# ReGLU MLP on one core: the first two chunks' first matmuls interleaved, and the second matmuls two chunks behind

## The chip, the cores and the metric

The kernel runs on one core of a Trainium2 chip. The metric is the device time of one execution in microseconds (us). The time before is the median of 6 runs, 356.47 us (355.37 to 356.92).

## What is computed

The input x has 16 x 256 = 4096 rows of 512 numbers. All inputs and the output are float32.

```python
h = x @ w1                              # w1: 512 x 4096
gate, value = np.split(h, 2, axis=-1)   # 2048 columns each
h = np.maximum(gate, 0) * value
return (h @ w2).astype(np.float32)      # w2: 2048 x 512
```

## The kernel before, in words

The 4096 rows are cut into 8 chunks of 512 rows (`T_CHUNK`, `NC`), each chunk into 4 blocks of 128 rows (`NB`). All matmuls are in bf16. The work of a chunk has two parts.

- MM1 (`mm1_pair`, L120 to L148) makes the hidden layer transposed, 128 hidden columns at a time. A pair is 4 matmuls of 128x512 into `val_ps` (L124) and 4 into `gate_ps` (L132); ScalarE copies `val_ps` to SBUF (L140), and VectorE makes max(gate, 0) * value and writes it as bf16 into `g_sb` (L141). A chunk has 16 pairs, 128 matmuls.
- MM2 (`mm2_block`, L150) makes one block of 128 output rows: 16 matmuls of 128x512 into `out_ps` (L154), a copy by ScalarE (L162), a store issued by SP (L163). A chunk has 4 blocks, 64 matmuls. The very last block is split into two halves of 256 columns (L166 to L180).

MM1 needs x transposed (`xt_sb`). It comes in two ways. For the first three chunks (`N_PE`), SP loads float32 blocks (`xf_sb`, L74), TensorE transposes each block in 4 pieces against a float32 identity (L102), and VectorE copies the result to `xt_sb` as bf16 (L105); this is `pe_transpose_block`. The four blocks of chunk 0 stand ahead of all MM1; the eight of chunks 1 and 2 are placed one behind each of the pairs 1 to 8 of chunk 0 (`pe_xpose_after_pair`, L192). For the chunks 3 to 7, POOL issues a DMA that casts the chunk to bf16 in DRAM (L109), and SP issues 4 transposing DMAs (L114). The cast is traced two chunks ahead of its use, the transposes one chunk ahead.

The weights are loaded and cast to bf16 by DMAs that POOL issues: w1 in ten pieces (L81; four of 256 columns, gate and value in turn, then six of 512), then w2 in four (L95). The w1 piece that holds the value columns of pairs 0 and 1 is the second. POOL makes the two identities (L53 to L56) ahead of these DMAs. Twelve small transposes of the bf16 identity (L68) go to TensorE at the very start.

The order of work: within a chunk all 16 pairs, then MM2 of the chunk before (L214). So MM2 of the last chunk comes at the end. The code is traced in this order, and a planner (the tile framework) puts each engine's instructions into the order in which they are issued: program order is the priority, but an instruction whose inputs are there earlier, by the planner's own reckoning, may be put ahead. It also places all semaphores. Each engine then works in its order; a wait holds everything behind it on that engine. A tile pool with n buffers makes the tile n later wait until the earlier one is read: `xtpool` and `gpool` have 3 buffers, the PSUM pools 2 per tile.

```python
for c in range(NC):
    ...
    for pr in range(NH):
        mm1_pair(xt_tiles[c], g_tiles[c], pr)
        if c == 0 and pr in pe_xpose_after_pair:
            k, b = pe_xpose_after_pair[pr]
            pe_transpose_block(xt_tiles[k], xf_tiles[k], b)
    if c >= 1:
        for b in range(NB):
            mm2_block(g_tiles[c - 1], c - 1, b)
```

Of the kernel before, what the change touches and what calls it, by code (L numbers as in the profile page):

```python
# [11 lines left out]
def kernel(  # L12
# [7 lines left out]
    nc = tc.nc  # L20
    P = 128
    dt = mybir.dt
    fp32 = dt.float32
    bf16 = dt.bfloat16

    x2 = x.flatten_outer_dims()
    out2 = out.flatten_outer_dims()
    T, D = x2.shape
    D2, J = w1.shape
    H, DO = w2.shape  # L30
    assert D2 == D and J == 2 * H and DO == D

    ND = D // P
    NH = H // P
    T_CHUNK = 512
    NC = T // T_CHUNK
    NB = T_CHUNK // P
    N_PE = 3
    N_WARMUP = 12

    const = ctx.enter_context(tc.tile_pool(name="const", bufs=1))
    wpool = ctx.enter_context(tc.tile_pool(name="wpool", bufs=1))
    xfpool = ctx.enter_context(tc.tile_pool(name="xfpool", bufs=N_PE))
    xtpool = ctx.enter_context(tc.tile_pool(name="xtpool", bufs=3))
    gpool = ctx.enter_context(tc.tile_pool(name="gpool", bufs=3))
    vpool = ctx.enter_context(tc.tile_pool(name="vpool", bufs=3))
    opool = ctx.enter_context(tc.tile_pool(name="opool", bufs=4))
    dram = ctx.enter_context(tc.tile_pool(name="dram", bufs=NC, space=bass.MemoryType.DRAM))
    ps_mm1 = ctx.enter_context(tc.tile_pool(name="ps_mm1", bufs=2, space=bass.MemoryType.PSUM))
    ps_mm2 = ctx.enter_context(tc.tile_pool(name="ps_mm2", bufs=2, space=bass.MemoryType.PSUM))  # L50
    ps_xt = ctx.enter_context(tc.tile_pool(name="ps_xt", bufs=2, space=bass.MemoryType.PSUM))

    ident_bf = const.tile([P, P], bf16)  # L53
    make_identity(nc, ident_bf)
    ident_f32 = const.tile([P, P], fp32)
    make_identity(nc, ident_f32)  # L56

    w1_sb = wpool.tile([P, ND, J], bf16)
    w2_sb = wpool.tile([P, NH, DO], bf16)

    w1_v = w1.rearrange("(dc p) j -> p dc j", p=P)
    w2_v = w2.rearrange("(hc p) n -> p hc n", p=P)
    x_v = x2.rearrange("(c b p) d -> c p b d", p=P, b=NB)
    out_v = out2.rearrange("(c b p) d -> c p b d", p=P, b=NB)

    warm = ps_xt.tile([P, ND, P], bf16, name="ps_xt")
    for i in range(N_WARMUP):
        nc.tensor.transpose(warm[:, i % ND, :], ident_bf, ident_bf)  # L68

    xf_tiles = {}  # L70
    for c in range(N_PE):
        xf = xfpool.tile([P, NB, D], fp32, name="xf_sb")
        for b in range(NB):
            nc.sync.dma_start(out=xf[:, b, :], in_=x_v[c, :, b, :])  # L74
        xf_tiles[c] = xf

    JQ = J // 8
    HQ = JQ // 2

    def load_w1_cols(j0, width):  # L80
        nc.gpsimd.dma_start(  # L81
            out=w1_sb[:, :, j0:j0 + width],
            in_=w1_v[:, :, j0:j0 + width],
        )
# [2 lines left out]
    load_w1_cols(4 * JQ, HQ)  # L87
    load_w1_cols(0 * JQ + HQ, HQ)
    load_w1_cols(4 * JQ + HQ, HQ)
    for q in (1, 2, 3):  # L90
        load_w1_cols(q * JQ, JQ)
        load_w1_cols((4 + q) * JQ, JQ)

    for h0 in range(0, NH, 4):
        nc.gpsimd.dma_start(  # L95
            out=w2_sb[:, h0:h0 + 4, :], in_=w2_v[:, h0:h0 + 4, :]
        )

    def pe_transpose_block(xt_tile, xf_tile, b):
        ps = ps_xt.tile([P, ND, P], fp32, name="ps_xt")  # L100
        for dc in range(ND):
            nc.tensor.transpose(  # L102
                ps[:, dc, :], xf_tile[:, b, dc * P:(dc + 1) * P], ident_f32
            )
        nc.vector.tensor_copy(out=xt_tile[:, :, b * P:(b + 1) * P], in_=ps)  # L105

    def emit_cast_chunk(c):
        xbf = dram.tile([T_CHUNK, D], bf16, name="x_bf16")
        nc.gpsimd.dma_start(out=xbf, in_=x2[c * T_CHUNK:(c + 1) * T_CHUNK, :])  # L109
        return xbf  # L110

    def emit_transpose_chunk(xbf, xt_tile):
        for dc in range(ND):
            nc.sync.dma_start(  # L114
                out=xt_tile[:, dc, :],
                in_=xbf[:, dc * P:(dc + 1) * P],
                transpose=True,
            )

    def mm1_pair(xt_tile, g_tile, pr):  # L120
        gate_ps = ps_mm1.tile([P, T_CHUNK], fp32, name="gate_ps")
        val_ps = ps_mm1.tile([P, T_CHUNK], fp32, name="val_ps")
        for dc in range(ND):
            nc.tensor.matmul(  # L124
                val_ps,
                w1_sb[:, dc, H + pr * P:H + (pr + 1) * P],
                xt_tile[:, dc, :],
                start=(dc == 0),
                stop=(dc == ND - 1),
            )  # L130
        for dc in range(ND):
            nc.tensor.matmul(  # L132
                gate_ps,
                w1_sb[:, dc, pr * P:(pr + 1) * P],
                xt_tile[:, dc, :],
                start=(dc == 0),
                stop=(dc == ND - 1),
            )
        val_sb = vpool.tile([P, T_CHUNK], fp32, name="val_sb")
        nc.scalar.copy(out=val_sb, in_=val_ps)  # L140
        nc.vector.scalar_tensor_tensor(  # L141
            out=g_tile[:, pr, :],
            in0=gate_ps,
            scalar=0.0,
            in1=val_sb,
            op0=mybir.AluOpType.max,
            op1=mybir.AluOpType.mult,
        )  # L148

    def mm2_block(g_tile, c, b, split_tail=False):  # L150
        if not split_tail:
            out_ps = ps_mm2.tile([P, DO], fp32, name="out_ps")
            for hc in range(NH):
                nc.tensor.matmul(  # L154
                    out_ps,
                    g_tile[:, hc, b * P:(b + 1) * P],
                    w2_sb[:, hc, :],
                    start=(hc == 0),
                    stop=(hc == NH - 1),
                )  # L160
            o_sb = opool.tile([P, DO], fp32, name="o_sb")
            nc.scalar.copy(out=o_sb, in_=out_ps)  # L162
            nc.sync.dma_start(out=out_v[c, :, b, :], in_=o_sb)  # L163
        else:
            DH = DO // 2
            for h in range(2):  # L166
                out_ps = ps_mm2.tile([P, DO], fp32, name="out_ps")
                for hc in range(NH):
                    nc.tensor.matmul(  # L169
                        out_ps[:, h * DH:(h + 1) * DH],  # L170
                        g_tile[:, hc, b * P:(b + 1) * P],
                        w2_sb[:, hc, h * DH:(h + 1) * DH],
                        start=(hc == 0),
                        stop=(hc == NH - 1),
                    )
                o_sb = opool.tile([P, DH], fp32, name="o_sb_half")
                nc.scalar.copy(out=o_sb, in_=out_ps[:, h * DH:(h + 1) * DH])  # L177
                nc.sync.dma_start(
                    out=out_v[c, :, b, h * DH:(h + 1) * DH], in_=o_sb
                )  # L180

    xt_tiles = {}
    g_tiles = {}
    xbf_tiles = {}

    xt_tiles[0] = xtpool.tile([P, ND, T_CHUNK], bf16, name="xt_sb")
    for b in range(NB):
        pe_transpose_block(xt_tiles[0], xf_tiles[0], b)
    for k in range(1, N_PE):
        xt_tiles[k] = xtpool.tile([P, ND, T_CHUNK], bf16, name="xt_sb")  # L190

    pe_xpose_after_pair = {}  # L192
    for k in range(1, N_PE):
        for b in range(NB):
            pe_xpose_after_pair[(k - 1) * NB + b + 1] = (k, b)

    for c in range(NC):
        k = c + 2
        if N_PE <= k < NC:
            xbf_tiles[k] = emit_cast_chunk(k)  # L200
        nxt = c + 1
        if N_PE <= nxt < NC:
            xt_tiles[nxt] = xtpool.tile([P, ND, T_CHUNK], bf16, name="xt_sb")
            emit_transpose_chunk(xbf_tiles[nxt], xt_tiles[nxt])

        g_tiles[c] = gpool.tile([P, NH, T_CHUNK], bf16, name="g_sb")

        for pr in range(NH):
            mm1_pair(xt_tiles[c], g_tiles[c], pr)
            if c == 0 and pr in pe_xpose_after_pair:  # L210
                k, b = pe_xpose_after_pair[pr]
                pe_transpose_block(xt_tiles[k], xf_tiles[k], b)

        if c >= 1:  # L214
            for b in range(NB):
                mm2_block(g_tiles[c - 1], c - 1, b)
            del g_tiles[c - 1]

    for b in range(NB):
        mm2_block(g_tiles[NC - 1], NC - 1, b, split_tail=(b == NB - 1))  # L220


# [28 lines left out]
```

## Time and profile before

| What | Value |
|---|---|
| median of 6 runs | 356.47 us (355.37 to 356.92) |
| the profiled execution | 357.17 us |
| its span, first to last instruction | 355.4 us |
| mean granted TensorE clock | 0.999 |
| MM1 and MM2 matmuls in the kernel | 1536 |
| one MM1 copy on ScalarE (L140) | 586 ns, 128 times |
| one MM1 product on VectorE (L141) | 691 ns, 128 times |
| x blocks loaded by SP | 12, of 256 KB |
| stores of 256 KB by SP, issue to landing | 31, median 2.0 us |
| w1 pieces, issue to landing | 10, median 20.1 us |
| x casts by DMA (L109), issue to landing | 5, 19.6 to 20.0 us |

How to read it: the span is shorter than the execution's own time, which also holds what lies before the first and behind the last instruction. PE is TensorE, PEld its weight loads (beside the matmuls), DVE VectorE, ACT ScalarE, POOL GpSimd, and SP the engine that only issues DMAs. "x12" after a row is the number of instructions. The times of a chain or timeline row are its start and its length in us from the start of the span. A matmul's own duration in the profile (about 380 ns) is longer than the step from one matmul to the next, because matmuls overlap in the array; the steps are what counts. q1 is the queue of the DMAs that SP issues, q0 that of POOL's.

### The profile page before, as it was taken

To read this page: it belongs to the slowest core of one execution; us is meant where nothing else is said; L and a number is where in the kernel's file an instruction comes from. 1 tells how busy PE (TensorE), PEld (TensorE's weight loads), DVE (VectorE), ACT (ScalarE), POOL (GpSimd) and SP (SyncE) were. 2 spreads that over 40 slices of the span, in tenths; PEclk is the share of its full clock that TensorE was granted. 3 is DMA by queue.
4 is the path that set the end of the run, shared out by engine and by line. 5 is a ranking of instruction groups with operands and counts; after the bars stand their busy time and mean duration, and the time that the engine had idled before them with its cause. 6 is when DMAs were issued, how large, how long until landed. Compare 5 with 4: busy or idle time off the path is not lost.

```text
span 355.4 us, 3970 instructions
## 1 busy us (share of the span) xinstructions
PE 342.6 (96%) x1581; PEld 160.7 (45%) x1612; DVE 96.1 (27%) x140; ACT 95.2 (27%) x162; POOL 14.1 (4%) x27
## 2 busy tenths in 40 slices
PE   5599999999999999999999999999999999999996
PEld 4245444444444444444444444444444444444444
DVE  2145434420333104330144203341033301442000
ACT  1022333321333123321333213331233213332111
POOL 8132000000000000000000000000000000000000
PEclk9999999999999999999999999999999999999999
DMA  8999994023000320004100130000200011000212
GB/s 201 280 206 207 229 226 71 1 34 116 30 0 2 89 89 2 0 3 117 59 0 2 39 108 32 1 0 31 89 0 2 0 59 61 0 0 2 89 60 87
DMA packets 24929, 23.31 MB, mean 66 GB/s; under 512 B 11904, under 2 KB 19328, under 8 KB 24832
## 3 DMA queue, kind: packets, MB, share of 16 engines
q0 software_dynamic: 7552, 8.91, 14.5%
q1 hardware_dynamic: 17360, 14.16, 13.2%
q8 instruction: 12, 0.20, 0.2%
q14 instruction: 5, 0.04, 0.0%
HBM read 20.97 MB, written 11.01 MB: 90 GB/s over the span
## 4 chain that ended last, share of the span: by engine, by line
PE 95%; DMA 3%; issue 1%; POOL 0%; ACT 0%; POOLq 0%
PE val_ps L124 31%; PE gate_ps L132 31%; PE out_ps L154 30%; DMA w_sb<-in_w_dram 3%; PE out_ps L169 1%; PE ps_xt L102 1%; POOL w_sb L81 0%; ACT o_sb_half L177 0%; POOL ident_bf masks.py:199 0%; POOL ident_f_92 masks.py:199 0%; POOL ident_f_92 masks.py:197 0%; POOL ident_bf masks.py:197 0%; POOLq L235 0%
## 5 line engine op out<-in xcount | busy, mean ns | idle before, releaser
L141 DVE SCALAR_TENSOR_TENSOR g_sb<-gate_ps,val_sb 128x512 bf16<-128x512 f32 x128 | 88.5, 691 | 221.0 <-PE gate_ps L132 215.8
L124 PE MATMUL val_ps<-xt_sb,w_sb 128*128 128x512 bf16 x502 | 131.6, 383 | 4.1 <-DMA w_sb<-in_w_dram 3.7
L132 PE MATMUL gate_ps<-xt_sb,w_sb 128*128 128x512 bf16 x500 | 131.1, 382 | 0.7
L140 ACT COPY val_sb<-val_ps 128x512 f32<-128x512 f32 x128 | 75.0, 586 | 158.9 <-PE val_ps L124 151.7
L154 PE MATMUL out_ps<-w_sb,g_sb 128*128 128x512 bf16 x487 | 107.7, 379 | 0.5
L124 PEld LDWEIGHTS <-w_sb 128*128 128x128 bf16 x512 | 50.4, 99 | 63.7 <-DMA w_sb<-in_w_dram 4.1
L132 PEld LDWEIGHTS <-w_sb 128*128 128x128 bf16 x512 | 50.5, 99 | 61.5 <-issue 1.9
L154 PEld LDWEIGHTS <-g_sb 128*128 128x128 bf16 x496 | 48.5, 98 | 58.5
L162 ACT COPY o_sb<-out_ps 128x512 f32<-128x512 f32 x31 | 18.2, 586 | 95.0 <-PE out_ps L154 91.2
L102 PE MATMUL ps_xt<-ident_f_92,xf_sb 128*128 128x128 f32 x48 | 9.4, 336 | 2.5 <-DMA xf_sb<-in_x_dram 2.5
L105 DVE CAST xt_sb<-ps_xt 128x512 bf16<-128x512 f32 x12 | 8.2, 685 | 7.9 <-PE ps_xt L102 7.9
L102 PEld LDWEIGHTS ps_xt<-ident_f_92,xf_sb 128*128 128x128 f32 x48 | 7.2, 173 | 5.2 <-DVE xt_sb L105 2.5
L81 POOL DMA_DIRECT2D w_sb<-in_w_dram x10 | 7.6, 785 | 6.1 <-DMA w_sb<-in_w_dram 6.1
L169 PE MATMUL out_ps<-w_sb,g_sb 128*128 128x256 bf16 x32 | 3.7, 273 | 0.0
L169 PEld LDWEIGHTS <-g_sb 128*128 128x128 bf16 x32 | 3.1, 98 | 0.6
L95 POOL DMA_DIRECT2D w_sb<-in_w_dram x4 | 3.0, 740 | 6.6 <-DMA w_sb<-in_w_dram 6.6
L68 PE MATMUL ps_xt<-ident_bf 128*128 128x128 bf16 x12 | 1.5, 312 | 1.5 <-POOL ident_bf masks.py:199 1.5
L68 PEld LDWEIGHTS <-ident_bf 128*128 128x128 bf16 x12 | 1.2, 144 | 1.5 <-POOL ident_bf masks.py:199 1.5
L140 ACT ACT_TABLE_LOAD x1 | 1.3, 1283 | 0.7 <-PEq L235 0.7
L177 ACT COPY o_sb_half<-out_ps 128x256 f32<-128x256 f32 x2 | 0.7, 372 | 2.5 <-PE out_ps L169 2.5
L109 POOL DMA_DIRECT2D x_bf_425<-in_x_dram x1 | 0.5, 532 | 1.8 <-DMA w_sb<-in_w_dram 1.8
L109 POOL DMA_DIRECT2D x_bf_716<-in_x_dram x1 | 0.5, 502 | 2.0 <-DMA w_sb<-in_w_dram 2.0
(11 smaller groups left out, 2.8 us busy)
## 6 DMA issues: line engine op xcount, KB each, us to landing
out_dram<-o_sb SPq DMA_DIRECT2D x31, 256.0 KB, 2.0
w_sb<-in_w_dram POOLq DMA_DIRECT2D x10, 512.0 KB, 20.1
xf_sb<-in_x_dram SPq DMA_DIRECT2D x12, 256.0 KB, 7.8
w_sb<-in_w_dram POOLq DMA_DIRECT2D x4, 256.0 KB, 13.0
x_bf_425<-in_x_dram POOLq DMA_DIRECT2D x1, 512.0 KB, 20.0
x_bf_716<-in_x_dram POOLq DMA_DIRECT2D x1, 512.0 KB, 19.9
x_bf_1012<-in_x_dram POOLq DMA_DIRECT2D x1, 512.0 KB, 19.8
x_bf_1308<-in_x_dram POOLq DMA_DIRECT2D x1, 512.0 KB, 19.6
```

The lines of the kernel that those rows point to most:

```text
L68: nc.tensor.transpose(warm[:, i % ND, :], ident_bf, ident_bf)
L81: nc.gpsimd.dma_start(out=w1_sb[:, :, j0:j0 + width], in_=w1_v[:, :, j0:j0 + width],)
L95: nc.gpsimd.dma_start(out=w2_sb[:, h0:h0 + 4, :], in_=w2_v[:, h0:h0 + 4, :])
L102: nc.tensor.transpose(ps[:, dc, :], xf_tile[:, b, dc * P:(dc + 1) * P], ident_f32)
L105: nc.vector.tensor_copy(out=xt_tile[:, :, b * P:(b + 1) * P], in_=ps)
L124: nc.tensor.matmul(val_ps, w1_sb[:, dc, H + pr * P:H + (pr + 1) * P], xt_tile[:, dc, :], start=(dc == 0), stop=(dc == ND - 1),)
L132: nc.tensor.matmul(gate_ps, w1_sb[:, dc, pr * P:(pr + 1) * P], xt_tile[:, dc, :], start=(dc == 0), stop=(dc == ND - 1),)
L140: nc.scalar.copy(out=val_sb, in_=val_ps)
L141: nc.vector.scalar_tensor_tensor(out=g_tile[:, pr, :], in0=gate_ps, scalar=0.0, in1=val_sb, op0=mybir.AluOpType.max, op1=mybir.AluOpType.mult,
L154: nc.tensor.matmul(out_ps, g_tile[:, hc, b * P:(b + 1) * P], w2_sb[:, hc, :], start=(hc == 0), stop=(hc == NH - 1),)
L162: nc.scalar.copy(out=o_sb, in_=out_ps)
L169: nc.tensor.matmul(out_ps[:, h * DH:(h + 1) * DH], g_tile[:, hc, b * P:(b + 1) * P], w2_sb[:, hc, h * DH:(h + 1) * DH], start=(hc == 0), s ...
```

## The change

- MM1 of the chunks 0 and 1 is traced pair by pair in turn: pair 0 of chunk 0, pair 0 of chunk 1, pair 1 of chunk 0, and so on. All eight blocks of both chunks are transposed by TensorE ahead of it in the program. Chunks 2 to 7 get x by cast and transposing DMAs; the six casts are all traced at the start, behind w1 and ahead of w2, on POOL's queue.
- MM2 follows two chunks behind: chunk c's MM1, then MM2 of chunk c - 2. At the end stand MM2 of chunks 6 and 7.
- The bf16 identity and the twelve small transposes go. Eight matmuls of 128x512 on a zeroed tile take their place; VectorE zeroes it. The float32 identity is made on POOL behind the first four w1 DMAs.
- `mm2_block` is written without the two branches; its matmuls, copies and stores are the same.

The diff, cut to its core:

```diff
-    N_PE = 3
-    N_WARMUP = 12
+    N_JOINT = 2
+    N_WARMUP = 8
...
-    ident_bf = const.tile([P, P], bf16)
-    make_identity(nc, ident_bf)
-    ident_f32 = const.tile([P, P], fp32)
-    make_identity(nc, ident_f32)
...
+    dummy = const.tile([P, DO], bf16)
+    nc.vector.memset(dummy, 0.0)
+    warm_ps = ps_mm2.tile([P, DO], fp32, name="out_ps")
+    for i in range(N_WARMUP):
+        nc.tensor.matmul(warm_ps, dummy[:, :P], dummy, start=True, stop=True)
...
-    warm = ps_xt.tile([P, ND, P], bf16, name="ps_xt")
-    for i in range(N_WARMUP):
-        nc.tensor.transpose(warm[:, i % ND, :], ident_bf, ident_bf)
...
-    for c in range(N_PE):
+    for c in range(N_JOINT):
...
     load_w1_cols(4 * JQ + HQ, HQ)
+
+    ident_f32 = const.tile([P, P], fp32)
+    make_identity(nc, ident_f32)
+
     for q in (1, 2, 3):
         load_w1_cols(q * JQ, JQ)
         load_w1_cols((4 + q) * JQ, JQ)
+
+    xbf_tiles = {}
+    for c in range(N_JOINT, NC):
+        xbf = dram.tile([T_CHUNK, D], bf16, name="x_bf16")
+        nc.gpsimd.dma_start(out=xbf, in_=x2[c * T_CHUNK:(c + 1) * T_CHUNK, :])
+        xbf_tiles[c] = xbf
...
+    for c in range(N_JOINT):
         for b in range(NB):
-            pe_xpose_after_pair[(k - 1) * NB + b + 1] = (k, b)
...
+            pe_transpose_block(xt_tiles[c], xf_tiles[c], b)
+
+    if N_JOINT < NC:
+        xt_tiles[N_JOINT] = xtpool.tile([P, ND, T_CHUNK], bf16, name="xt_sb")
+        emit_transpose_chunk(xbf_tiles[N_JOINT], xt_tiles[N_JOINT])
+
+    for c in range(N_JOINT):
+        g_tiles[c] = gpool.tile([P, NH, T_CHUNK], bf16, name="g_sb")
+    for pr in range(NH):
+        for c in range(N_JOINT):
+            mm1_pair(xt_tiles[c], g_tiles[c], pr)
+
+    for c in range(N_JOINT, NC):
         nxt = c + 1
-        if N_PE <= nxt < NC:
+        if nxt < NC:
...
-            if c == 0 and pr in pe_xpose_after_pair:
-                k, b = pe_xpose_after_pair[pr]
-                pe_transpose_block(xt_tiles[k], xf_tiles[k], b)
-
-        if c >= 1:
+
+        cc = c - 2
+        if cc >= 0:
             for b in range(NB):
-                mm2_block(g_tiles[c - 1], c - 1, b)
-            del g_tiles[c - 1]
-
-    for b in range(NB):
-        mm2_block(g_tiles[NC - 1], NC - 1, b, split_tail=(b == NB - 1))
+                mm2_block(g_tiles[cc], cc, b)
+            del g_tiles[cc]
+
+    for cc in range(NC - 2, NC):
+        for b in range(NB):
+            mm2_block(g_tiles[cc], cc, b, split_tail=(cc == NC - 1 and b == NB - 1))
```

More of the change, by code (lines that the diff above doesn't have):

```diff
@@ L37 @@
     NB = T_CHUNK // P
-    N_PE = 3
-    N_WARMUP = 12
+    N_JOINT = 2
+    N_WARMUP = 8
     const = ctx.enter_context(tc.tile_pool(name="const", bufs=1))
     wpool = ctx.enter_context(tc.tile_pool(name="wpool", bufs=1))
-    xfpool = ctx.enter_context(tc.tile_pool(name="xfpool", bufs=N_PE))
+    xfpool = ctx.enter_context(tc.tile_pool(name="xfpool", bufs=N_JOINT))
     xtpool = ctx.enter_context(tc.tile_pool(name="xtpool", bufs=3))
@@ L51 @@
     ps_xt = ctx.enter_context(tc.tile_pool(name="ps_xt", bufs=2, space=bass.MemoryType.PSUM))
-    ident_bf = const.tile([P, P], bf16)
-    make_identity(nc, ident_bf)
-    ident_f32 = const.tile([P, P], fp32)
-    make_identity(nc, ident_f32)
+    dummy = const.tile([P, DO], bf16)
[3 more added lines that the diff above has]
+        nc.tensor.matmul(warm_ps, dummy[:, :P], dummy, start=True, stop=True)
+    x_v = x2.rearrange("(c b p) d -> c p b d", p=P, b=NB)
+    out_v = out2.rearrange("(c b p) d -> c p b d", p=P, b=NB)
+    xf_tiles = {}
+    for c in range(N_JOINT):
+        xf = xfpool.tile([P, NB, D], fp32, name="xf_sb")
+        for b in range(NB):
+            nc.sync.dma_start(out=xf[:, b, :], in_=x_v[c, :, b, :])
+        xf_tiles[c] = xf
     w1_sb = wpool.tile([P, ND, J], bf16)
@@ L62 @@
     w2_v = w2.rearrange("(hc p) n -> p hc n", p=P)
-    x_v = x2.rearrange("(c b p) d -> c p b d", p=P, b=NB)
-    out_v = out2.rearrange("(c b p) d -> c p b d", p=P, b=NB)
-    warm = ps_xt.tile([P, ND, P], bf16, name="ps_xt")
-    for i in range(N_WARMUP):
-        nc.tensor.transpose(warm[:, i % ND, :], ident_bf, ident_bf)
-    xf_tiles = {}
-    for c in range(N_PE):
-        xf = xfpool.tile([P, NB, D], fp32, name="xf_sb")
-        for b in range(NB):
-            nc.sync.dma_start(out=xf[:, b, :], in_=x_v[c, :, b, :])
-        xf_tiles[c] = xf
     JQ = J // 8
@@ L105, in pe_transpose_block @@
         nc.vector.tensor_copy(out=xt_tile[:, :, b * P:(b + 1) * P], in_=ps)
[L107 to L110, printed above, removed]
     def emit_transpose_chunk(xbf, xt_tile):
@@ L150, in mm2_block @@
     def mm2_block(g_tile, c, b, split_tail=False):
-        if not split_tail:
+        nsplit = 2 if split_tail else 1
+        DW = DO // nsplit
+        for h in range(nsplit):
             out_ps = ps_mm2.tile([P, DO], fp32, name="out_ps")
@@ L154, in mm2_block @@
                 nc.tensor.matmul(
-                    out_ps,
+                    out_ps[:, h * DW:(h + 1) * DW],
                     g_tile[:, hc, b * P:(b + 1) * P],
-                    w2_sb[:, hc, :],
+                    w2_sb[:, hc, h * DW:(h + 1) * DW],
                     start=(hc == 0),
@@ L160, in mm2_block @@
                 )
[L161 to L180, printed above, removed]
+            o_sb = opool.tile([P, DW], fp32, name="o_sb", tag="o_sb")
@@ L182 @@
+            nc.scalar.copy(out=o_sb, in_=out_ps[:, h * DW:(h + 1) * DW])
+            nc.sync.dma_start(
+                out=out_v[c, :, b, h * DW:(h + 1) * DW], in_=o_sb
+            )
     xt_tiles = {}
     g_tiles = {}
[L184 to L192, printed above, removed]
@@ L193 @@
-    for k in range(1, N_PE):
-        for b in range(NB):
-            pe_xpose_after_pair[(k - 1) * NB + b + 1] = (k, b)
[L197 to L200, printed above, removed]
+    for c in range(N_JOINT):
+        xt_tiles[c] = xtpool.tile([P, ND, T_CHUNK], bf16, name="xt_sb")
+    for c in range(N_JOINT):
+        for b in range(NB):
+            pe_transpose_block(xt_tiles[c], xf_tiles[c], b)
+    if N_JOINT < NC:
+        xt_tiles[N_JOINT] = xtpool.tile([P, ND, T_CHUNK], bf16, name="xt_sb")
+        emit_transpose_chunk(xbf_tiles[N_JOINT], xt_tiles[N_JOINT])
@@ L201 @@
+    for c in range(N_JOINT):
+        g_tiles[c] = gpool.tile([P, NH, T_CHUNK], bf16, name="g_sb")
+    for pr in range(NH):
+        for c in range(N_JOINT):
+            mm1_pair(xt_tiles[c], g_tiles[c], pr)
+    for c in range(N_JOINT, NC):
         nxt = c + 1
-        if N_PE <= nxt < NC:
+        if nxt < NC:
             xt_tiles[nxt] = xtpool.tile([P, ND, T_CHUNK], bf16, name="xt_sb")
@@ L209 @@
             mm1_pair(xt_tiles[c], g_tiles[c], pr)
-            if c == 0 and pr in pe_xpose_after_pair:
-                k, b = pe_xpose_after_pair[pr]
-                pe_transpose_block(xt_tiles[k], xf_tiles[k], b)
-        if c >= 1:
+        cc = c - 2
+        if cc >= 0:
             for b in range(NB):
-                mm2_block(g_tiles[c - 1], c - 1, b)
-            del g_tiles[c - 1]
-    for b in range(NB):
-        mm2_block(g_tiles[NC - 1], NC - 1, b, split_tail=(b == NB - 1))
+                mm2_block(g_tiles[cc], cc, b)
+            del g_tiles[cc]
+    for cc in range(NC - 2, NC):
+        for b in range(NB):
+            mm2_block(g_tiles[cc], cc, b, split_tail=(cc == NC - 1 and b == NB - 1))
 _INS = ['x', 'w1', 'w2']
```

## The prediction

> **What bounds the kernel now.** I read the busy shares first, then the chain of work that ended last, then the first 40 us of that chain, the timeline and the DMA queues there.
>
> ```profile
> PE 342.6 (96%) x1581; PEld 160.7 (45%) x1612; DVE 96.1 (27%) x140; ACT 95.2 (27%) x162; POOL 14.1 (4%) x27
> ...
> PE 95%; DMA 3%; issue 1%; POOL 0%; ACT 0%; POOLq 0%
> ```
>
> TensorE is busy 96% of the span and is 95% of the chain; the only other piece of size is 3% of DMA. VectorE and ScalarE are idle 73% of the time. So the kernel can only get shorter by PE work taken out, by an earlier start or by a shorter slow stretch at the start. The opening of the chain (start us, us, what):
>
> ```profile
> 1.66 0.87 POOL w_sb L81
> 2.52 11.81 DMA w_sb<-in_w_dram
> 14.33 0.05 issue
> 14.38 1.89 PE val_ps L124 x4
> 16.26 1.71 PE gate_ps L132 x4
> 17.97 1.71 PE val_ps L124 x4
> 19.68 1.08 PE gate_ps L132 x4
> ...
> 22.49 0.44 PE ps_xt L102 x4
> ...
> 35.47 0.44 PE ps_xt L102 x4
> ```
>
> Three costs stand here. (1) The first real matmul starts at 14.38, released by the second w1 DMA, issued at 2.52. (2) The first 16 matmuls take 14.38 to 20.76, 6.38 us, where 16 at the later pace take 3.45: in the chain MM1 of a later chunk runs 172.31 to 199.94 (128 matmuls) and MM2 199.94 to 213.75 (64), both 0.2158 us each. The first 14 stand 0.427 us apart, half speed for about 5.9 us, which costs 2.93 us; the granted-clock row says 1.00 there, so only the pace shows it. (3) Seven x blocks are transposed inside chunk 0, 22.49 to 35.47, at 0.436 us each: 3.05 us.
>
> The whole account: 14.38 + 1520 x 0.2158 (328.0) + 3.51 for the 32 half-width matmuls of the last block + 2.93 + 3.05 = 351.9; the chain's PE part ends at 348.43 + 3.51 = 351.94. Then 3.46 us of copy and store to 355.4. Nothing is left unexplained, so from 36 us on there is no stall to remove. The profiled execution took 357.17, 1.77 more than its span; the median of the runs is 356.47. I take differences of the span over to the median.
>
> **Part by part.**
>
> *MM2 lagging by two chunks, and the joint order of chunks 0 and 1.* The same 1536 matmuls with the same weight loads; a pair's weights are still loaded anew for each chunk. MM1 to MM2 has no wait now (idle before L154 is 0.5 us in all), so a longer lag has nothing to hide: 0. Each pair still gives PE 1.73 us against 0.586 (ScalarE copy) and 0.691 (VectorE product) with the same two PSUM buffers: 0. g(3) takes the buffer of g(0), which MM2(0) has read just before MM1(3) in PE order: 0. If that cover went, one drain of about 1 us per chunk would show.
>
> *w1 demand.* Now pair 4 starts at 24.93 and its value columns landed at 24.21, when POOL was released: 0.7 us of margin. In the joint order a pair lasts 3.45 us, so pair 4 is asked for at about 14 + 13.8 + 3 = 31 us, some 7 us after 24.2. No gain, since nothing waited, but more margin.
>
> *Casts of x moved up, ahead of w2 on POOL's queue, and one more of them; four more DMA transposes on SP.* POOL issues the ninth and later transfers as earlier ones land; its issue times 26.72, 29.27, 31.81, 34.36, 36.89 give 2.55 us per transfer. The last w1 landed near 34.4. Six casts at 2.5 us end near 50, w2's four near 60. MM2(0) asks for w2 at about 14 + 384 x 0.2158 + 3 = 100: hidden by 40 us. xt(2) now comes by DMA transposes that wait on SP for the first cast, about 37; the first such group here took from its issue at 48.0 to about 58.6, so it lands near 48 and is asked for at 72. xt(3) waits on SP for chunk 0 to end and has MM1(2) and MM2(0), 41 us, before it is needed. Behind these waits on SP stand only output stores, the first due near 101. All 0 within these covers; the edge would be a w2 or xt 24 us late.
>
> *ident_bf and twelve small transposes out; a memset and eight 512-wide matmuls in; ident_f32 behind four w1 issues.* The dummies run from about 1.1 at the half pace, 8 x 0.427 = 3.4, to 4.5. POOL's w1 issues take 0.90 and three times 0.76 from 0.74, so ident_f32 is ready near 3.9 + 0.5 = 4.4, 0.75 later than the first block's start at 3.65. Two blocks then take 1.94, to 6.5, and the third x block lands at 7.3. Hidden, by 0.8 us.
>
> *When the first real matmul starts.* Now w1 is issued 0.9 us earlier (0.74 against 1.63), and SP loads eight x blocks, not twelve. The x blocks pace the transposes, as these rows show (the next two are of the timeline, the last four of the DMA queues from 0 to 12 us and from 0 to 14 us: packets, MB, share):
>
> ```profile
> 7.35 3.31 PE L102 MATMUL ps_xt<-ident_f_92,xf_sb 128*128 128x128 f32 x12 [1.73 <-DMA xf_sb<-in_x_dram]
> ...
> 14.61 0.74 POOL L81 DMA_DIRECT2D w_sb<-in_w_dram  x1 [3.21 <-DMA w_sb<-in_w_dram]
> ```
> ```profile
> q1 hardware_dynamic: 1205, 2.21, 60.9%
> q0 software_dynamic: 1001, 0.50, 31.5%
> ```
> ```profile
> q1 hardware_dynamic: 1468, 2.69, 62.4%
> q0 software_dynamic: 1264, 0.63, 33.8%
> ```
>
> From 12 to 14 us x (q1) moves 0.24 MB/us and w1 (q0) 0.065. The eighth x block was issued at 4.1 and landed 8.6 later, 12.7. Does x give way to the earlier w1? The Trainium skill's "DMA: Bandwidth & Descriptors", section "Issuing engines are not separate DMA queues", says that transfers from all engines share the same 16 engines and only the issue time is saved, which speaks against moving w1 up. By that rule alone, what w1 gains x loses. The rows price it: in the 0.9 us x falls from about 0.30 MB/us (302 GB/s in the 2 to 4 us window, x alone) to 0.24, losing 0.054 MB or 0.2 us. So the last x block lands near 12.95, its four transposes at the slow pace take about 1.05 (the blocks of 7.35 to 10.66 are 1.1 apart), and PE is free at 14.0. The second w1 DMA, 14.33 less 0.9, lands near 13.4; after 12 us it no longer shares with x (the third chunk's megabyte is gone), so not later.
>
> Which comes first on PE? The order is the planner's, not quite the program's: here block (1,0) was put ahead of pair 0, and (1,1) left behind pair 2 where the code has it. So it believes that w1 lands about with the sixth x block, and may put some matmuls of chunk 0 ahead of the last three or four blocks. Both ends: all eight blocks first, start 14.0 and nothing inside, sum 14.0; or start 13.4 with three blocks (1.31) or four (1.74) behind it, 14.7 to 15.1. Before it is 14.38 + 3.05 = 17.43. The gain is 3.4 at one end and 2.3 at the other; with neither order shown I take 3.0, nearer to the first because transposes have the earlier place in the program.
>
> *The half-speed stretch.* Can the eight dummies spare it? They end near 4.5, and up to 14 only f32 transposes run, about 0.85 of every 1.06 us, while x lands. The Trainium skill, "TensorE: Matmul & The Clock Gate", Part 4 "PE-mode transpose", says that transposes don't count as busy for the clock; its Part 1 says that an idle window of about 3.4 us returns the array to half speed. By these the dummies are wasted and 2.93 us stays. The page's other figure, about 3.4 us of slow work, would already give only 1.7 us of loss now; the trace has 5.9 us slow, and the measurement decides. No row shows the array after dense dummies and transposes at 80%. Both ends: 0 saved, or all 2.93. I take 0, by the row that is nearest: nine us of transposes with gaps left the array slow at 14.38.
>
> *The end.* Same split last block, same copy and store: 3.46 us stays.
>
> Sum: span 355.4 - 3.0 = 352.4, profiled execution about 354.2, median 356.47 - 3.0 = 353.5.
>
> **Rivals.** *Likeliest, 0.58:* as summed, 353.5, within 352.5 to 354.6 (gains 2.3 to 3.4, and some tenths for the slow stretch, whose length is seen once while the runs spread 1.55 us).
>
> *The array is at full speed when MM1 starts, 0.20.* Eight dummies and two blocks of transposes are 5.3 us without a gap, then transposes fill 80%. If that counts as work, most of 2.93 is saved too: gain 5.9, 350.5 (to 351.5 if partly). Against it: the slow start at 14.38 after 3.3 us of such transposes, with 3.7 us of idling between.
>
> *The change doesn't do what it is for, 0.13.* Four blocks sit behind the first matmuls while the array is slow, cost 1.06 each, and lengthen the slow stretch by not counting: 13.4 + 4.24 + 2.93 = 20.6 against 17.43 + 2.93 = 20.36. Gain -0.2 to 0.9: 356.1.
>
> *Slower, 0.09.* PE takes work in order, so no matmul passes the eighth block; before, only the fifth stood ahead. If the earlier w1 takes half of x's pace, 0.12 MB/us from 3.7 on with 0.55 MB done, 2.1 MB are moved at 16.6, the block lands at 17.6 and MM1 starts at 18.7. It decides from a start at 17.43, a landing of 16.4. Price: 18.7 - 17.43 = 1.3, so 357.8. Against it: the queue rows, where x keeps 0.24 MB/us beside w1.
>
> **Numbers.** About 0.3% (1.07 us) is what a measurement of this kernel can tell from no change: below 355.4 is faster, above 357.5 slower. The first two cases are faster, with some of the third: 0.80. Same 0.12, slower 0.08. The range, 350.0 to 355.6, takes in the full-speed case and the likeliest with its orders, and leaves out most of the last two.
>
> **What would show it.** Right: first MM1 matmul at 13.3 to 14.2; none or few ps_xt rows after it; some 14 matmuls 0.427 apart; chunk 1's MM1 ending near 72; no PE idle time on w1, w2 or xt; last matmul near 349. Matmuls at 0.216 from the start mean the second case; ps_xt rows 1.06 apart between slow matmuls the third; a start past 17.4 that waits on xf_sb the last. I am wrong in kind if PE stands still anywhere after 20 us.

## The result and the profile after

The changed kernel takes 353.64 us (median of 10 runs, 350.63 to 354.40), the kernel before 356.56 us in the runs beside it: a ratio of 0.9907, 95% interval 0.9886 to 0.9928. That is 2.9 us less; the forecast was 353.5. But the runs of the kernel before spread over 1.8 us and those of the changed one over 3.8, and the execution whose profile follows is one of the short ones: 351.15 us with a span of 349.4. So the profile alone would mislead about the median, and the spread has to be explained too. (Of the experiments below, one execution of e6, at 611.66 us with a mean granted clock of 0.569, is left out.)

Busy shares and the chain by engine, as before nearly all PE:

```profile
PE 339.8 (97%) x1561; PEld 157.4 (45%) x1592; DVE 94.3 (27%) x137; ACT 95.0 (27%) x162; POOL 14.2 (4%) x26
...
PE 95%; DMA 3%; issue 1%; POOL 0%; ACT 0%; ACTq 0%; POOLq 0%
```

The opening of the chain that ended last (start us, us, what):

```profile
1.23 0.87 POOL w_sb L78
2.10 9.97 DMA w_sb<-in_w_dram
12.07 0.05 issue
12.11 0.39 PE val_ps L126
12.50 0.44 PE ps_xt L109 x4
12.94 0.22 PE val_ps L126
13.16 0.56 PE ps_xt L109 x4
13.71 0.43 PE val_ps L126 x2
14.14 0.86 PE gate_ps L134 x4
```

MM1 starts at 12.11, not 14.38; two x blocks stand between its first matmuls, not seven further on; and the four gate matmuls take 0.86 from the start where those of before took 1.71. The DMA queues from 0 to 12 us:

```profile
q1 hardware_dynamic: 1128, 2.08, 55.9%
q0 software_dynamic: 1236, 0.62, 39.4%
```

x (q1) has moved 0.13 MB less than before by 12 us, w1 (q0) 0.12 MB more. The end is longer, though. In the DMA view from 344.6 us, the last half-width store lands after 2.7 us, with an instruction load (q14) beside it; the store of before took 1.7:

```profile
q14 instruction: 1, 0.01, 0.4%
...
out_dram<-o_sb SPq DMA_DIRECT2D x1, 128.0 KB, 2.7
```

The account of the prediction, made again for five traces. The loss is what remains of PE's end when start, 331.5 us of matmuls and the blocks (0.436 each) are taken off; the tail runs from PE's end to the end of the span. All in us.

| Kernel | start of MM1 | blocks inside | loss at half speed | tail | span | median of its runs |
|---|---|---|---|---|---|---|
| before | 14.38 | 7: 3.05 | 2.93 | 3.46 | 355.4 | 356.5 |
| changed | 12.11 | 2: 0.87 | 0.37 | 4.55 | 349.4 | 353.64 |
| e8, same order at the start | 13.74 | 2: 0.87 | 2.67 | 4.02 | 352.8 | 354.18 |
| e9, before with N_PE = 2 | 13.43 | 3: 1.31 | 2.85 | 3.41 | 352.5 | 353.98 |
| e12, fillers and own tile | 13.67 | 0 | 0.02 | 3.41 | 348.6 | 350.42 |

### The profile page after: what moved, and what is told of

It reads as the page before. It is cut to its first block, busy times and chain, and to the rows that moved or that the text cites. A ratio compares the mean times of both kernels' runs of the same rounds, so it can differ in the third digit from the quotient of the medians.

```text
span 349.4 us, 3922 instructions
## 1 busy us (share of the span) xinstructions
PE 339.8 (97%) x1561; PEld 157.4 (45%) x1592; DVE 94.3 (27%) x137; ACT 95.0 (27%) x162; POOL 14.2 (4%) x26
## 3 DMA queue, kind: packets, MB, share of 16 engines
q1 hardware_dynamic: 18960, 13.64, 13.4%
## 4 chain that ended last, share of the span: by engine, by line
PE 95%; DMA 3%; issue 1%; POOL 0%; ACT 0%; ACTq 0%; POOLq 0%
PE val_ps L126 32%; PE out_ps L158 31%; PE gate_ps L134 31%; DMA w_sb<-in_w_dram 3%; PE ps_xt L109 0%; POOL w_sb L78 0%; ACT o_sb L166 0%; ACTq L166 0%; POOLq L223 0%
## 5 line engine op out<-in xcount | busy, mean ns | idle before, releaser
L134 PE MATMUL gate_ps<-xt_sb,w_sb 128*128 128x512 bf16 x498 | 129.6, 379 | 0.4
L158 PE MATMUL out_ps<-w_sb,g_sb 128*128 128x512 bf16 (+1 forms) x517 | 111.0, 373 | 0.6
L166 ACT COPY o_sb<-out_ps 128x512 f32<-128x512 f32 (+1 forms) x33 | 18.9, 572 | 96.7 <-PE out_ps L158 96.7
L109 PE MATMUL ps_xt<-ident_f_114,xf_sb 128*128 128x128 f32 x32 | 6.3, 353 | 1.6 <-POOL ident_f_114 masks.py:199 0.9
L112 DVE CAST xt_sb<-ps_xt 128x512 bf16<-128x512 f32 x8 | 5.5, 692 | 7.8 <-PE ps_xt L109 7.7
L109 PEld LDWEIGHTS ps_xt<-ident_f_114,xf_sb 128*128 128x128 f32 x32 | 4.8, 180 | 3.9 <-POOL ident_f_114 masks.py:199 1.8
L57 PE MATMUL out_ps<-dummy 128*128 128x512 bf16 x8 | 3.6, 631 | 1.2 <-DVE dummy L54 1.2
L57 PEld LDWEIGHTS <-dummy 128*128 128x128 bf16 x8 | 1.0, 140 | 2.8 <-issue 1.7
L98 POOL DMA_DIRECT2D x_bf_135<-in_x_dram x1 | 0.5, 488 | 2.9 <-DMA w_sb<-in_w_dram 2.9
L98 POOL DMA_DIRECT2D x_bf_133<-in_x_dram x1 | 0.5, 488 | 2.1 <-DMA w_sb<-in_w_dram 2.1
L98 POOL DMA_DIRECT2D x_bf_129<-in_x_dram x1 | 0.5, 486 | 2.1 <-DMA w_sb<-in_w_dram 2.1
L98 POOL DMA_DIRECT2D x_bf_131<-in_x_dram x1 | 0.5, 486 | 2.0 <-DMA w_sb<-in_w_dram 2.0
L98 POOL DMA_DIRECT2D x_bf_125<-in_x_dram x1 | 0.5, 532 | 0.9 <-DMA w_sb<-in_w_dram 0.9
```

Of the source, the lines that this page charges most:

```text
L57: nc.tensor.matmul(warm_ps, dummy[:, :P], dummy, start=True, stop=True)
L109: nc.tensor.transpose(ps[:, dc, :], xf_tile[:, b, dc * P:(dc + 1) * P], ident_f32)
L134: nc.tensor.matmul(gate_ps, w1_sb[:, dc, pr * P:(pr + 1) * P], xt_tile[:, dc, :], start=(dc == 0), stop=(dc == ND - 1),)
L158: nc.tensor.matmul(out_ps[:, h * DW:(h + 1) * DW], g_tile[:, hc, b * P:(b + 1) * P], w2_sb[:, hc, h * DW:(h + 1) * DW], start=(hc == 0), s ...
L166: nc.scalar.copy(out=o_sb, in_=out_ps[:, h * DW:(h + 1) * DW])
```

## The experiments

After the result I held theory A: the eight dummies bring the array to full speed in part of the executions. Its rivals were that they do nothing, and that the gain comes from the order of MM2.

**e1, no dummies.**

```diff
-    dummy = const.tile([P, DO], bf16)
-    nc.vector.memset(dummy, 0.0)
...
-        nc.tensor.matmul(warm_ps, dummy[:, :P], dummy, start=True, stop=True)
```

> The changed kernel without the zeroed tile and its eight matmuls. Theory A (the dummies are what makes the array run at full speed when MM1 starts, in part of the executions): no execution is fast any more, the lowest rises from 350.6 to 352 or more, median 353.5 to 354.5, and the profile shows the first MM1 matmuls 0.427 us apart. Rival (the dummies do nothing; transposes or chance decide): the same spread, 350.6 to 354.4, median 353.6.

Measured: 353.68 (350.98 to 355.29), the same as with them, ratio 0.9911 (0.9881 to 0.9942). Theory A fell as an account of the spread. The timeline of TensorE (start us, us; the last row shown is the first gate group):

```profile
5.67 3.87 PE L104 MATMUL ps_xt<-ident_f,xf_sb 128*128 128x128 f32 x16 [5.67 <-POOL ident_f masks.py:199]
9.70 1.79 PE L104 MATMUL ps_xt<-ident_f,xf_sb 128*128 128x128 f32 x8 [0.16 <-DMA xf_sb<-in_x_dram]
12.88 0.39 PE L121 MATMUL val_ps<-xt_sb,w_sb 128*128 128x512 bf16 x1 [1.39 <-DMA w_sb<-in_w_dram]
13.11 0.60 PE L104 MATMUL ps_xt<-ident_f,xf_sb 128*128 128x128 f32 x4
...
14.63 1.03 PE L129 MATMUL gate_ps<-xt_sb,w_sb 128*128 128x512 bf16 x4
```

PE had done nothing but transposes, 16 of them in 3.87 us and 8 more, and yet MM1 begins at full speed at 12.88: the next instruction stands 0.23 us behind its first matmul, not 0.427.

**e2, sixteen dummies.**

```diff
-    N_WARMUP = 8
+    N_WARMUP = 16
```

> The changed kernel with sixteen dummies in place of eight. Theory A: more than 5 us of dense work without a gap bring the array to full speed in every execution, the transposes behind it keep it there, and MM1 starts at full speed: median 350.5 to 351.3, spread under 1.5 us. Rival (transposes with gaps let it fall back before MM1): median 353.6 to 354.2, first MM1 matmuls 0.427 us apart.

Measured: 353.42 (350.47 to 354.98), the same spread again. More work at the very start is not what is missing.

**e3, the kernel before with sixteen wide dummies.**

```diff
-        nc.tensor.transpose(warm[:, i % ND, :], ident_bf, ident_bf)
+        nc.tensor.matmul(warm_ps, dummy[:, :P], dummy, start=True, stop=True)
```

> The kernel before with sixteen wide dummies in place of its twelve small transposes, nothing else. Here PE stands still for 3.7 us ahead of MM1. Theory A with the idle time as the breaker: the array is slow again at MM1, median 356.2 to 356.8 as before. Rival (once at full speed it stays so over the gap): the slow stretch of 2.9 us goes, median 353.8 to 354.5.

Measured: 356.22, ratio 0.9989 (0.9974 to 1.0004): no change that can be told. Here a row shows what happens. This is the busy time of the w1 and w2 instructions by stretches (PE, PEld, POOL, then the granted clock, DMA share and GB/s):

```profile
8.00:12.00 4.00, 0.38 (x1) 0.10 (x1) 0.75 (x1) 1.00 1.19 305
12.00:16.00 4.00, 2.23 (x6) 0.87 (x7) 0.74 (x1) 0.74 1.21 291
16.00:24.00 8.00, 7.40 (x31) 2.94 (x30) 2.91 (x4) 0.92 1.28 205
```

PE waits 2.43 us for w1 ahead of 13.77. The granted clock is 1.00 until 12 and 0.74 on average over the next 4 us; in finer stretches it is 1.00 up to 13.5 and 0.50 from 14, so it falls at the end of this wait. In the kernel before the row said 1.00 all along, although its first matmuls went at half the pace: the row shows a fall, but not an array that has not yet risen.

**e4, the kernel before with MM2 two chunks behind.**

```diff
-        if c >= 1:
+        if c >= 2:
             for b in range(NB):
-                mm2_block(g_tiles[c - 1], c - 1, b)
+                mm2_block(g_tiles[c - 2], c - 2, b)
```

> The kernel before with MM2 two chunks behind and nothing else. My theory (MM2 never waited, so the lag is worth nothing): 356.5, within 0.4. Rival (the lag is part of the gain): 355.5 or less.

Measured: 356.61, ratio 1.0006 (0.9989 to 1.0023). The lag is worth nothing.

From e1 to e3 came theory B: in the changed order the array usually rises while the blocks are transposed, and in many executions it falls back in the pauses ahead of MM1.

**e5, fillers in the pauses.**

```diff
             pe_transpose_block(xt_tiles[c], xf_tiles[c], b)
+            k, e = (c, b - 1) if b else (c - 1, NB - 1)
+            for i in range(n_fill.get((c, b), 0)):
+                nc.tensor.matmul(
+                    warm_ps, dummy[:, :P], xt_tiles[k][:, :, e * P:(e + 1) * P],
+                    start=True, stop=True,
+                )
```

> The changed kernel with ten more dummy matmuls among the last x blocks: two behind blocks (0,3) and (1,0) each, six behind (1,1), each reading an already transposed x block so that the planner can't put them earlier; the transposes of (1,2) and (1,3) then stand ahead of MM1. Theory B (the array reaches full speed on the transposes in nearly every execution, but falls back in the pauses ahead of MM1 in more than half of them, which gives the 350.6 to 354.4 spread): the pauses are filled, all executions start MM1 at full speed, median 351.2 to 351.9, spread under 1.5 us. Rival (the spread comes from when x and w1 land, not from the array's speed): spread as before, 351 to 354.5, median 353.7 to 354.2.

Measured: 351.77 (350.96 to 353.27), ratio 0.9870 (0.9846 to 0.9893), 1.9 us below the changed kernel. The spread is 2.3 us, narrower than 3.8 but wider than I expected. The trace has one more fall: PE pauses from 4.7 to 5.7 us while POOL makes the identity and 0.78 us ahead of 7.53, and the granted clock is 0.50 from 8 to 10 us. It is 1.00 again from 12 us on, and MM1 starts late, at 14.68, but at full speed.

**e6 and e9, the kernel before with two chunks by TensorE.**

```diff
-    N_PE = 3
+    N_PE = 2
```

> The kernel before with two chunks instead of three by TensorE transposes (N_PE = 2), nothing else. My sum: four transposes fewer inside chunk 0 (1.74) and a megabyte of x less ahead of w1, first MM1 matmul near 13.4 instead of 14.38 (1.0), slow stretch as before: 353.5 to 354.2. Rival (the start is set by the order of w1, not by the amount of x): only the 1.74, 354.7.

> The same kernel as in the sixth experiment, for a profile and more executions. If taking the third chunk off TensorE is worth the whole gain: 353.1 to 353.6, first MM1 matmul near 13.2, three blocks inside chunk 0, the first matmuls 0.427 us apart. If its one look was chance: 354.5.

Measured: 353.24 and 353.98, ratios 0.9911 (0.9893 to 0.9929) and 0.9928 (0.9911 to 0.9944). e6 fell below its forecast (353.5 to 354.2), e9 came out above its own (353.1 to 353.6). The profile of e6 is that of the execution left out, so the chain is that of e9:

```profile
2.53 10.86 DMA w_sb<-in_w_dram
13.38 0.04 issue
13.43 1.89 PE val_ps L124 x4
15.32 1.71 PE gate_ps L132 x4
17.02 1.71 PE val_ps L124 x4
18.73 0.93 PE gate_ps L132 x4
```

This one number took off 3.2 and 2.5 us against the runs beside it, about what the whole change gave at the median (2.9): an earlier start (0.95) and four blocks fewer (1.74), with the first matmuls at half speed as before. In this trace the granted clock had fallen to 0.50 near 8.5 us, behind a pause of 2.81 us; the five other executions of e9 have a mean granted clock of 1.000 and are as long, so there the row shows no fall, as in the kernel before.

**e7, the identity ahead of w1.**

```diff
+    ident_f32 = const.tile([P, P], fp32)
+    make_identity(nc, ident_f32)
+
     xf_tiles = {}
...
-    ident_f32 = const.tile([P, P], fp32)
-    make_identity(nc, ident_f32)
-
     for q in (1, 2, 3):
```

> The changed kernel with the float32 identity traced ahead of the first w1 DMA. Theory: w1 leaves POOL some tenths later and lands 0.3 to 0.5 later, transposes start at once behind the dummies: median 353.6 to 354.1. Rival (the identity behind the w1 DMAs costs, since it keeps PE idle near 5 us): 353.2 or less.

Measured: 354.56 (352.56 to 355.95), ratio 0.9940 (0.9919 to 0.9961): 0.9 above the changed kernel, but the two intervals overlap, so it stays unclear whether the order counts. The forecast of 353.6 to 354.1 missed too, and the rival is out. MM1 starts at 13.62 and at half speed; the granted clock fell near 9.8 us, almost 4 us earlier, and the longest pause of PE until then was 1.25 us.

**e8, no interleaving.**

```diff
-    for pr in range(NH):
-        for c in range(N_JOINT):
+    for c in range(N_JOINT):
+        for pr in range(NH):
             mm1_pair(xt_tiles[c], g_tiles[c], pr)
```

> The changed kernel with all pairs of chunk 0 ahead of those of chunk 1, so that only the interleaving is undone. My theory (w1 lands fast enough for one chunk at a time, with 0.7 us or more to spare): 353.6, within 0.6. Rival (the interleaving is what spares w1 waits): 354.5 or more, with PE idle on w1 in the trace.

Measured: 354.18 (350.38 to 354.56), ratio 0.9912 (0.9877 to 0.9947). No PE wait on w1 stands in the trace after the first matmul, so interleaving is worth nothing that can be told. The instructions up to the end of pair 0 are those of the changed kernel, so this trace shows what the other kind of execution of it is like. The stretches (PE, PEld, DVE, ACT, POOL, granted clock, DMA share, GB/s), and then the chain:

```profile
8.00:10.00 2.00, 0.91 (x7) 0.47 (x5) 0.95 (x2) 0.00 (x0) 0.00 (x0) 1.00 1.21 292
10.00:12.00 2.00, 1.14 (x8) 0.84 (x8) 1.13 (x2) 0.00 (x0) 0.65 (x1) 0.96 1.22 294
12.00:14.00 2.00, 0.51 (x3) 0.26 (x2) 0.69 (x1) 0.00 (x0) 0.12 (x2) 0.50 1.38 220
14.00:16.00 2.00, 2.00 (x9) 1.59 (x8) 0.69 (x1) 0.00 (x0) 1.25 (x2) 0.50 1.34 203
16.00:18.00 2.00, 2.00 (x8) 0.83 (x7) 0.69 (x1) 0.58 (x1) 0.51 (x1) 0.50 1.25 207
18.00:20.00 2.00, 1.95 (x8) 0.88 (x8) 0.69 (x1) 0.17 (x1) 0.49 (x1) 0.83 1.24 206
```
```profile
13.74 0.61 PE val_ps L126
14.35 0.85 PE ps_xt L109 x4
15.21 0.43 PE val_ps L126
15.63 0.85 PE ps_xt L109 x4
16.48 0.85 PE val_ps L126 x2
17.34 1.59 PE gate_ps L134 x4
```

PE is busy for half of 8 to 12 us and a quarter of 12 to 14. The granted clock falls to 0.50 near 11.9 (0.86 on average from 11.5 to 12), ahead of the pause of 1.49 us that ends with MM1 at 13.74. The two blocks between the matmuls then cost 0.85 each in place of 0.44.

So theory B has the place of the fall wrong: in e8 and e7 it lies among the x blocks, before the last pause. And that pause alone does not bring it: in the trace of e2 it is longer, 1.92 us, the clock stays at 1.00, and MM1 starts at full speed:

```profile
13.61 0.39 PE L126 MATMUL val_ps<-xt_sb,w_sb 128*128 128x512 bf16 x1 [1.92 <-DMA w_sb<-in_w_dram]
...
15.35 1.03 PE L134 MATMUL gate_ps<-xt_sb,w_sb 128*128 128x512 bf16 x4
```

The transposes ahead of it differ as well. In the trace of the changed kernel they begin slowly and fill PE, in that of e8 they begin fast and then wait for x and for VectorE's copies (0.72 to 0.91 us ahead of each of the next three blocks):

```profile
5.66 3.86 PE L109 MATMUL ps_xt<-ident_f_114,xf_sb 128*128 128x128 f32 x16 [0.87 <-POOL ident_f_114 masks.py:199]
```
```profile
5.66 1.10 PE L109 MATMUL ps_xt<-ident_f,xf_sb 128*128 128x128 f32 x8 [0.87 <-POOL ident_f masks.py:199]
```

From 6 to 12 us PE is busy 4.78 us in the first and 3.14 in the second. So the eight dummies had the array fast by 5.66 in e8, and PE then ran out of work. That this thin stretch is what lets the array fall is argued, not shown: e2 began as fast (8 transposes in 1.04 us), was busy 4.29 us from 6 to 12, and kept its speed.

The record has the mean granted clock of every execution, and it sorts them. Of the 11 executions of the changed kernel the three shortest (350.63 to 351.15) have 0.997 or 0.998. Seven of the other eight (352.42 to 354.40) have 0.985 to 0.995, so their clock fell for some time; one (353.81) has 0.999, which would fit an array that had not risen yet. e2 splits in the same way: four executions of 350.47 to 352.34 at 0.999 or 1.000, four of 354.50 to 354.98 at 0.989 to 0.995.

**e10, e6 with fillers.** Twelve of them, two behind block 2 and ten behind block 3 of chunk 0.

```diff
+    n_fill = {2: 2, 3: 10}
     for b in range(NB):
         pe_transpose_block(xt_tiles[0], xf_tiles[0], b)
+        for i in range(n_fill.get(b, 0)):
+            nc.tensor.matmul(
+                warm_ps, dummy, xt_tiles[0][:, :, (b - 1) * P:b * P],
+                start=True, stop=True,
+            )
```

> The kernel before with two chunks by TensorE and twelve dummy matmuls that read transposed blocks of chunk 0, two behind block 2 and ten behind block 3, in the pause ahead of MM1 (block (1,0) then falls behind pair 1: four blocks inside instead of three, 0.44). Theory B (a filled pause spares the slow start, whatever the rest of the order): 353.2 + 0.4 less some 1.5 to 2.2, 351.4 to 352.1. Rival (the slow start is a matter of the real matmuls only): 353.6 or more.

Measured: 351.94 (351.28 to 353.82), ratio 0.9877 (0.9855 to 0.9900): the fillers help in the old order too, as theory B has it. MM1 starts at 13.62 at full speed.

**e11, more dummies, fillers spread.**

```diff
-    N_WARMUP = 8
+    N_WARMUP = 11
...
-    n_fill = {(0, 3): 2, (1, 0): 2, (1, 1): 6}
+    n_fill = {(0, 2): 1, (0, 3): 1, (1, 0): 2, (1, 1): 4}
```

> The fifth experiment with eleven dummies at the start, to bridge to the first transposes, and the eight fillers spread over blocks (0,2) to (1,1). Theory B: full speed by 8 us in every execution and no pause long enough to lose it: 350.6 to 351.3, with the first MM1 matmul near 13.5. Rival (what is left in the fifth is the landing of x, not the speed): 351.7 as there.

Measured: 351.84 (350.95 to 353.09), as e5; the forecast of 350.6 to 351.3 failed. The trace is at full speed from 5.66 us on, with a start at 13.57 and a span of 349.2, so what holds the median up does not show in it. The two longest executions (352.24 and 353.09) have a mean granted clock of 0.997 and 0.995, the others 0.999 or 1.000.

**e12, e11 with a tile of its own for the half-width stores.**

```diff
-            o_sb = opool.tile([P, DW], fp32, name="o_sb", tag="o_sb")
+            o_sb = opool.tile([P, DW], fp32, name="o_sb" if nsplit == 1 else "o_sb_half")
```

> The eleventh experiment with a tile of its own for the two half-width stores of the end, as in the kernel before. In all looks at kernels of the changed structure the last 128 KB store landed after 2.2 to 2.7 us, in all of the old structure after 1.7, and with an instruction load beside it. Theory (the instruction load near the end slows the last store): 2.2 or more stays, median 351.8. Rival (the half-width tile that shares the slot of the full one slows the store): 1.7, median 351.0 to 351.4.

Measured: 350.42 (350.32 to 351.26), ratio 0.9833 (0.9814 to 0.9851), the best of all and below the rival's 351.0 to 351.4; e11 has 0.9874 (0.9854 to 0.9895), taken on another chip with runs of the kernel before beside it. In the DMA view from 343.8 us the last stores land after 1.7 again, and no instruction load is left there:

```profile
q1 hardware_dynamic: 321, 0.30, 18.2%
...
out_dram<-o_sb_half SPq DMA_DIRECT2D x2, 128.0 KB, 1.7
```

The timeline of its start shows pauses of at most 0.34 us between 5.86 and MM1:

```profile
9.66 0.63 PE L109 MATMUL ps_xt<-ident_f,xf_sb 128*128 128x128 f32 x4 [0.34 <-DMA xf_sb<-in_x_dram]
10.13 0.59 PE L181 MATMUL out_ps<-xt_sb,dummy 128*128 128x512 bf16 x2
...
12.98 0.63 PE L109 MATMUL ps_xt<-ident_f,xf_sb 128*128 128x128 f32 x4 [0.24 <-DMA xf_sb<-in_x_dram]
13.67 0.81 PE L126 MATMUL val_ps<-xt_sb,w_sb 128*128 128x512 bf16 x3
14.31 1.03 PE L134 MATMUL gate_ps<-xt_sb,w_sb 128*128 128x512 bf16 x4
```

The instruction load vanished with the own tile. So the rival's 1.7 came, but whether the store is slowed by the load or by the shared slot can't be told from one edit that removed both.

## Why the prediction was right, and where not

The time, the direction and the bound (the start, and PE work inside chunk 0) were right. By steps:

- *MM2's lag and the joint order: 0.* Right: e4 shows it for the lag; for the order e8 shows no w1 wait and no difference that the spread lets one tell.
- *w1 demand, casts, w2, DMA transposes: hidden.* Right: in the trace after, the chain passes from MM1 to MM2 at 96.16 without a wait.
- *Fewer x blocks.* Right in kind: the planner did put matmuls of chunk 0 ahead of the last blocks, of two, not of three or four. That costs 0.87 where I had 0 to 1.74.
- *The start.* The last x block landed at 4.7 + 8.3 = 13.0, as worked out (12.95). The second w1 DMA was mis-sized: 12.1 in this trace, not 13.4, though POOL issued the first at 1.23, not 0.74, so only 0.4 earlier. In the traces of e1, e2, e7 and e8 MM1 starts at 12.88, 13.61, 13.62 and 13.74, so the landing moves by 1.6 us among kernels with nearly the same start, and 13.4 lies within.
- *The identity hidden by 0.8 us.* Wrong: it was ready near 5.6, because a fifth w1 DMA was put between its two instructions, and the first transposes came at 5.66. At the median nothing was lost by it.
- *The half-speed stretch: "I take 0, by the row that is nearest".* This is the step that failed in kind. The stretch is neither kept nor spared. Both happen: in the traces of e1, e2 and of the changed kernel it is gone (a loss of 0.37 us in the last), in those of e7 and e8 the array had risen and fell back ahead of MM1 (a loss of 2.67 in e8). The row taken as nearest had PE idle for 3.72 us ahead of 14.38, which the changed order does not have. The Trainium skill's "TensorE: Matmul & The Clock Gate", Part 4 "PE-mode transpose", says that full speed doesn't engage for transposes, which don't count as busy in the same way; e1 contradicts it, with 24 float32 transposes and nothing else ahead of a fast MM1. Its Part 1 has the array go back after an idle window of about 3.4 us; in e7 and e8 the clock fell although no pause had been longer than 1.25 us, and here the measurement decides.
- *The tail: 3.46 stays.* Wrong by 0.6 to 1.1: seven traces of the new structure end with a last store of 2.2 to 2.7 us, five at the old one with 1.7, and e12 puts it back.

So the 3.0 came out as the sum of errors that cancel, and that the median fell within 0.2 us of the forecast is in this part luck. With the start of e8, 14.38 - 13.74 and 3.05 - 0.87 give 2.8; the array spares up to 2.6 more in the other executions, and the tail takes back 0.6 or more. e6 and e9 show that the third chunk of x, taken off TensorE and off the queue ahead of w1, is alone worth as much as the whole change at the median. They don't show that the rest gave nothing: the speed of the array in part of the executions and the longer tail work against each other.

That the array's speed at MM1 makes the runs of the changed kernel spread is shown by the granted clock of the executions and by the fillers (e5, e10). What decides whether it falls in a given execution is open: the pause ahead of w1 is not enough (e2), and the thin stretch among the transposes is only argued. What is not settled either is why e11 lies 1.4 above e12 when its tail is 0.7 longer in the traces; a fall in its two longest executions can be part of it.

## What to carry to other kernels

When PE is 96% busy and has no stall later on, the start (here the first 36 us) holds nearly all that can be won: when the first operand pair lands, what is issued ahead of it, which work is put between the first matmuls, and whether the array is at full speed when they come. Dummies at the very start alone gave nothing here (e1, e2, e3); fillers tied by data to the last work before the wait gave 1.9 us (e5) and, in the old order, 1.3 to 2.0 (e10 against e6 and e9). When one edit bundles several ideas, try each alone: here a single constant, N_PE = 2, gave as much as the whole at the median.

## What was not expected

- Transposes alone bring the array to full speed (e1: 24 of them between 5.67 and 11.49 us). It can fall back with no pause above 1.25 us (e7, e8) and hold over one of 1.92 (e2).
- The granted-clock row says 1.00 for an array that has not yet risen (the kernel before: 0.427 us per matmul) and 0.50 for one that has fallen (e8). The pace of the matmuls is the safer sign.
- The tag that lets the half-width tile share the full one's slot goes with one more instruction load at the end and 0.5 to 1.0 us on the last store; which of the two slows the store is open.
